# One more buffer for the routing tiles, and two bias tiles staged in the token-row buffers

## The chip, the cores and the metric

The kernel runs on 1 core of one Trainium2 chip. The metric is the device time of one execution in microseconds (us). The time before is 1835.21 us, the median of 3 runs (1820.68, 1835.21 and 1837.70).

## The reference, cut to what matters

One layer over 512 tokens of width 1024: a mixer (sparse attention and a state-space branch), then a mixture of 32 experts, 4 for each token. The change lies where the mixer ends and the experts begin.

```python
logits = (hf @ w_router + b_router).astype(jnp.float32)
top_val, top_idx = lax.top_k(logits, TOP_K)           # 4 of 32 experts per token
gates = jax.nn.softmax(top_val, axis=-1)
...
xb = h_pad[toks]                                      # the rows of one expert, in blocks of 128
gu = xb @ w_gu[e] + b_gu[e]
g, u = gu[:, :D_EXPERT], gu[:, D_EXPERT:]
g = jnp.minimum(g, SWIGLU_LIMIT)
u = jnp.clip(u, -SWIGLU_LIMIT, SWIGLU_LIMIT)
act = (u + 1.0) * (g * jax.nn.sigmoid(SWIGLU_ALPHA * g))
out = act @ w_dn[e] + b_dn[e]                         # times the row's gate, then summed by token
...
x = x + g_f * moe
```

The last line's bias part does not need the experts' rows: for each token it is the sum over experts of gate times `b_dn[e]`, that is `gates @ b_dn`. The kernel computes it once for all four tiles of 128 tokens. These are the "shared-bias tiles".

## The kernel before, in words

All weights stream from HBM in tiles of 128x2048 f32 (1 MB). SyncE issues each load as soon as its buffer is free; there are ten buffers (six `raw2`, `B0`, `B1`, two `raw`). Each weight tile is split in two fp32r tiles by `msplit`: `hi` on ScalarE (L1318), `lo = raw - hi` on VectorE (L1319). A product is made of three matmuls (hi by hi, lo by hi, hi by lo; L1496 to L1498, for expert 0 L1353 to L1355). One expert takes 12 weight tiles: for each half f of its width two tiles for the gate half of `gu`, two for the up half, and two for a half of the down product.

For each expert e, GpSimd gathers its 128 rows of `h2d` in a tile `xg` (L1376, two buffers), by the indices `gi`; TensorE transposes them (L1270, `tr<-cst,xg`), ScalarE and VectorE make the hi and lo parts (`xh` L1271, `xl` L1273). After the gate and up products VectorE clips `u` (L1285) and makes `act` (L1286); TensorE transposes `act` (L1270, `tr<-cst,act`) for the down product. The down product of expert e-1 runs between the products of expert e; its result `y` (L1556, tag `y`, two buffers) is added to the output in HBM by an indirect accumulating DMA (`put`, L1289) with the row indices `si`.

The indices come from a routing step, done for groups of experts: `[0]`, `[1, 2]`, `[3]`, `[4..7]`, `[8..11]` and so on. Each group leaves four small tiles: `q`, `gi`, `si` and `gate`, allocated with the tags of the same names and `bufs=nbuf + 1`, which is 3 here. `si` of a group is read until the last `put` of its experts has landed. The group `[4..7]` is the fourth to be allocated and takes the buffer of group `[0]`; its `si` is written (L1248) at the end of the loop pass for e = 1, in which expert 0's `put` is issued.

The shared-bias tiles: `shared_biases` (L1390) loads `b_dn` to a `y` buffer and makes from it and the gates the two operands; `shared_down(t, ...)` (L1411) makes tile t: two matmuls (L1417, `dn<-ah,al`), two VectorE products with `gf` (L1418, `y<-dn,gf`), and one accumulating DMA to the output (L1419, `out_dram<-y`). Four tiles pass through the two `y` buffers, so tile 2 and tile 3 are written when the DMAs of tile 0 and 1 have landed. The row buffers `xg` are allocated in the order of the gathers: expert 0 in the first, expert 1 in the second, expert 2 in the first again.

What sets the order: a planner (the tile framework) puts the instructions of every engine in a fixed order when the kernel is built. It takes the earliest in program order among those that its own estimates hold to be ready. Within the loop over experts 1 to 32 the order on TensorE, VectorE and ScalarE is written out by hand (`tc.manual_schedule`); GpSimd's queue is the planner's throughout, and so is all of expert 0's part, which it may interleave with the beginning of expert 1's. On the chip every engine takes its instructions in that order and waits at each for what it needs.

In each hand-ordered pass for expert e and half f stand, in this order: gate product, a routing step, up product (with `u` and `act`), the transposes of half f of the next expert's rows, a routing step, the first half of the down product, the transposes of `act`, the second half of the down product.

`cmb` and `cmt` are two 128x128 bf16 mask tiles of the mixer, held in the pool `con` that lives to the end. The pool `W` lives as long as the mixer; the experts' pool `M` is placed on the memory that `W` leaves.

Of the kernel before, what the change touches and what calls it, by code (L numbers as in the profile page):

```python
# [13 lines left out]
BF = mybir.dt.bfloat16  # L14
I32 = mybir.dt.int32
# [7 lines left out]
P = 128  # L23
L = 512
NT = L // P
# [108 lines left out]
def program(tc, A, dbg=None, upto=99):  # L134
# [5 lines left out]
    with ctx:  # L140
# [15 lines left out]
            (0, 8), (8, 24), (24, 32), (32, 38), (38, 46), (46, 106), (106, 114)))  # L156
        identb = con.tile([P, P], BF, name="identb")
        V.tensor_copy(identb, ident)
        cmb = con.tile([P, P], BF, name="cmb")
        V.tensor_copy(cmb, cmask)  # L160
        ones = con.tile([P, P], F32, name="ones")
        V.memset(ones, 1.0)
        aux = con.tile([P, NT, NE, 6], BF, name="aux")
# [43 lines left out]
        with ExitStack() as c1:  # L207
# [53 lines left out]
            def weave(*lists, at=None):  # L261

                steps = [((i + (at[n] if at else 0.5)) / len(ls), n, i) for n, ls in enumerate(lists) for i in range(len(ls))]
                for _, n, i in sorted(steps):
                    lists[n][i]()


            def two(tag):
# [447 lines left out]
                    V.tensor_scalar(mask[:, qt - 1, 0:n], sc, -2e38, NEG, op0=OP.is_gt, op1=OP.mult)  # L716


            cmt = con.tile([P, P], BF, name="cmt")
            V.tensor_scalar(cmt, trile, -1.0, -NEG, op0=OP.add, op1=OP.mult)  # L720
            sts = big("V", [P, 4, L])
            v3 = lambda a: a.rearrange("p (h d) -> p h d", d=64)
# [501 lines left out]
        def block_parts(M, mp, nbuf):  # L1224
            def mt(shape, dt=F32, name="t", bufs=None):
                return M.tile(list(shape), dt, name=name, tag=name, bufs=bufs or nbuf)

            def picked(hots, name, bufs, c):
                n = len(hots)
                p = mp.tile([P, 512], F32, name=name, tag=name, bufs=bufs)[:, 0:3 * n].rearrange("p (e c) -> p e c", c=3)  # L1230
                for i, (hot, aux_of) in enumerate(hots):
                    for t in range(NT):
                        T.matmul(p[:, i, :], hot[:, t, :], aux_of(t)[:, c:c + 3], start=(t == 0), stop=(t == NT - 1))
                return p.rearrange("p e c -> p c e")

            def slots(hots):

                n = len(hots)
                q = mt([P, 8, n], name="q", bufs=nbuf + 1)
                V.tensor_copy(q[:, 0:3, :], picked(hots, "mi", 1, 0))  # L1240
                return rows_of(q, n)

            def rows_of(q, n):
                gi, si = mt([P, n], I32, name="gi", bufs=nbuf + 1), mt([P, n], I32, name="si", bufs=nbuf + 1)
                V.scalar_tensor_tensor(q[:, 6], q[:, 0], 128.0, q[:, 1], op0=OP.mult, op1=OP.add)
                V.tensor_copy(gi, q[:, 6])
                V.tensor_scalar(q[:, 7], q[:, 2], cm512, c512, op0=OP.mult, op1=OP.add)
                V.tensor_tensor(si, q[:, 6], q[:, 7], op=OP.add)  # L1248
                return q, gi, si

            def share(hots, q):
                V.tensor_copy(q[:, 3:6, :], picked(hots, "dn", 2, 3))
                return share_of(q, len(hots))

            def share_of(q, n):
                gate = mt([P, n], name="gate", bufs=nbuf + 1)
                V.tensor_tensor(gate, q[:, 3], q[:, 4], op=OP.add)
                V.tensor_tensor(gate, gate, q[:, 5], op=OP.add)
                return gate

            def transposed(src, name, split_=True, b=None, into=None, scale=1.0):
                if into is None:
                    hi = mt([P, KD, P], F32R if split_ else F32, name=name + "h", bufs=nbuf)
                    lo = mt([P, KD, P], F32R, name=name + "l", bufs=nbuf) if split_ else None
                else:
                    hi, lo = into
                for b in range(2) if b is None else (b,):
                    p = mp.tile([P, 4, P], F32, name="tr", tag="tr", bufs=2)
                    for k in range(4):
                        T.transpose(p[:, k, :], src[:, (4 * b + k) * P:(4 * b + k + 1) * P], ident)  # L1270
                    S.activation(hi[:, 4 * b:4 * b + 4, :], p, AF.Copy, scale=scale)  # L1271
                    if split_ and scale == 1.0:
                        V.tensor_tensor(lo[:, 4 * b:4 * b + 4, :], p, hi[:, 4 * b:4 * b + 4, :].bitcast(F32),  # L1273
                                        op=OP.subtract)
                    elif split_:
                        V.scalar_tensor_tensor(lo[:, 4 * b:4 * b + 4, :], p, scale,
                                               hi[:, 4 * b:4 * b + 4, :].bitcast(F32), op0=OP.mult, op1=OP.subtract)
                return hi, lo

            def gated(act, p):  # L1280
                S.activation(act, p, AF.Silu, scale=ALPHA)

            def upped(u, p, act):

                V.tensor_scalar(u, p, 8.0, -6.0, op0=OP.min, op1=OP.max)  # L1285
                V.scalar_tensor_tensor(act, act, SILU7, u, op0=OP.min, op1=OP.mult)  # L1286

            def put(y, si, out=out):
                return G.indirect_dma_start(out=out, out_offset=bass.IndirectOffsetOnAxis(ap=si, axis=0), in_=y,  # L1289
                                     in_offset=None, compute_op=OP.add)  # L1290

            def all_picked(p, i, hot, aux_of):
                for t in range(NT):
                    T.matmul(p[:, i, :], hot[:, t, :], aux_of(t), start=(t == 0), stop=(t == NT - 1))

            def all_of(p, n):
                q = mt([P, 8, n], name="q", bufs=nbuf + 1)
                V.tensor_copy(q[:, 0:6, :], p.rearrange("p e c -> p c e"))
                q, gi, si = rows_of(q, n)
                return gi, si, share_of(q, n)  # L1300

            return slots, share, transposed, gated, upped, put, all_picked, all_of

        with ExitStack() as c2:
# [19 lines left out]
            def mt(shape, dt=F32, name="t", bufs=2):  # L1324
                return M.tile(list(shape), dt, name=name, tag=name, bufs=bufs)
# [17 lines left out]
            def three(x, b, e, c0, tag, bufs):  # L1343

                p = mp.tile([P, 512], F32, name=tag, tag=tag, bufs=bufs)
                if b is not None:
                    half, c = divmod(c0, b.shape[1])
                    T.matmul(p, sel2[:, half, e:e + 1].to_broadcast([P, P]), b[:, c:c + 512], start=True, stop=False)
                for i in range(2):
                    hi, lo = weights()  # L1350
                    for k in range(4):
                        ws, kk = slice(k * 512, (k + 1) * 512), 4 * i + k
                        T.matmul(p, x[0][:, kk, :], hi[:, ws], start=(b is None and kk == 0), stop=False)  # L1353
                        T.matmul(p, x[0][:, kk, :], lo[:, ws], start=False, stop=False)
                        T.matmul(p, x[1][:, kk, :], hi[:, ws], start=False, stop=(kk == KD - 1))  # L1355
                return p
# [30 lines left out]
            def sized(name):  # L1387
                return spare[name].pop(0) if spare[name] else mt([P, D], name=name, bufs=2 if name == "y" else 1)
# [21 lines left out]

            def shared_down(t, gT, b):  # L1411

                y = sized("y")
                for n in range(2):
                    ns = slice(n * 512, (n + 1) * 512)
                    p = mp.tile([P, 512], F32, name="dn", tag="dn", bufs=2)
                    T.matmul(p, gT[:, t, :], b[:, ns], start=True, stop=True)  # L1417
                    V.tensor_tensor(y[:, ns], p, gf[:, ns], op=OP.mult)  # L1418
                G.dma_start(out[t * P:(t + 1) * P, :], y, accum_op=OP.add)  # L1419
# [33 lines left out]
            for f in range(2):  # L1453
                fs = slice(f * 512, (f + 1) * 512)
                u = mt([P, 512], name="u", bufs=1)
                gated(act[:, fs], three(xT, bias["b_gu"], 0, f * 512, "gu", 3))
                if f == 0:
                    shares()
                    gates_of([0])
                    gates_of(groups[0])  # L1460
                    for step in routed([3]):
                        step()
                upped(u, three(xT, bias["b_gu"], 0, FE + f * 512, "gu", 3), act[:, fs])
                if f == 0:
                    shared = shared_biases()
                    xT_next = transposed(xg, "x")
                    xg = gather(2)
                else:
                    for t in range(NT):
                        shared_down(t, *shared)  # L1470
                aT = transposed(act, "a", b=f, into=aT, scale=1.0 / ALPHA)
            few = mt([P, NE], name="few", bufs=1)
# [208 lines left out]
```

## Time and profile before

| | us |
|---|---|
| median of 3 runs | 1835.21 |
| the three runs | 1820.68, 1835.21, 1837.70 |
| the profiled execution | 1834.64 |
| its span, from first to last instruction | 1832.9 |
| TensorE busy | 1764.1 (96%) |
| VectorE busy | 1542.3 (84%) |
| ScalarE busy | 1074.0 (59%) |
| GpSimd busy | 194.1 (11%) |
| data moved by DMA | 527.24 MB, mean 288 GB/s |

The profiled execution's own time is 1.7 us above its span and 0.6 us below the median. The mixer takes about the first 620 us, expert 0 and the start of expert 1 some 70 us more, and from about 740 us on the experts follow one another at about 36 us each until the end. In the rows below PE is TensorE, DVE VectorE, ACT ScalarE, POOL GpSimd and SP SyncE; times are us from the start of the span. The idle time in brackets is that of the engine just before the instruction, with what released it.

### The profile page before, as it was taken

The page shows a single profiled execution, that of the slowest core. Times are in us where ns is not written, and L with a number is a line of the kernel's source. Part 1 is how long each engine was busy: PE and PEld are TensorE (multiplying, and loading weights), DVE is VectorE, ACT ScalarE, POOL GpSimd, SP SyncE. Part 2 cuts the span into 40 slices and gives each one's busy share as a digit, 9 for nine tenths or more (in the row PEclk, how much of TensorE's full clock was granted, in tenths as well). Part 3 has the DMA queues.
Part 4 walks back from the last instruction along what each step waited for, and adds up shares of the span by engine and source line. Part 5 has one row for each costly group of instructions (what it writes and reads, how often), then busy time and mean ns, then how long its engine had stood idle before and what let it go on. Part 6 is the DMA issues. An engine that isn't in the chain of part 4 may idle for free.

```text
span 1832.9 us, 22584 instructions
## 1 busy us (share of the span) xinstructions
PE 1764.1 (96%) x8536; PEld 1392.0 (76%) x8536; DVE 1542.3 (84%) x1886; ACT 1074.0 (59%) x1059; POOL 194.1 (11%) x115
## 2 busy tenths in 40 slices
PE   7999999999999788999999999999999999999997
PEld 3866877776778566787888888888888788788885
DVE  6486678875776787999999999999999999999996
ACT  3443433444323365677777777777677777777774
POOL 0000000000000110111211111111111111211112
PEclk9988999998899899999999999999999999999999
DMA  8242334432575588999999999999999999999993
GB/s 327 71 150 72 117 134 165 152 126 76 200 262 197 192 288 286 361 378 374 373 381 375 380 363 390 372 382 369 369 384 386 352 396 379 358 385 381 377 354 73
DMA packets 86599, 527.24 MB, mean 288 GB/s; under 512 B 10928, under 2 KB 11088, under 8 KB 32216
## 3 DMA queue, kind: packets, MB, share of 16 engines
q1 hardware_dynamic: 70552, 469.70, 66.4%
q0 software_dynamic: 15696, 55.97, 11.2%
q8 instruction: 68, 1.11, 0.2%
q14 instruction: 43, 0.35, 0.1%
q10 hardware_dynamic: 240, 0.10, 0.0%
HBM read 497.91 MB, written 30.45 MB: 288 GB/s over the span
## 4 chain that ended last, share of the span: by engine, by line
PE 86%; DVE 8%; DMA 3%; issue 2%; ACT 1%; POOL 0%; SPq 0%; DVEq 0%; POOLq 0%; ACTq 0%
PE gu L1498 12%; PE gu L1496 12%; PE gu L1497 12%; PE dn L1496 6%; PE dn L1498 6%; PE dn L1497 6%; PE mm L392 4%; PE mm L393 4%; PE mm L394 4%; PE tr L1270 3%; PE gu L1507 2%; PE ac L849 1%; PE at L821 1%; PE mm L384 1%; DVE wlo L1319 1%
## 5 line engine op out<-in xcount | busy, mean ns | idle before, releaser
L1319 DVE TENSOR_TENSOR wlo<-raw,whi 128x2048 fp32r<-128x2048 f32 x154 | 352.1, 2287 | 30.1 <-ACT whi L1318 30.0
L1319 DVE TENSOR_TENSOR mlo<-raw,mhi 128x2048 fp32r<-128x2048 f32 (+1 forms) x160 | 352.5, 2207 | 25.2 <-ACT mhi L1318 22.9
L1318 ACT ACTIVATE whi<-raw 128x2048 fp32r<-128x2048 f32 x154 | 296.1, 1923 | 128.3 <-PE gu L1498 68.0
L1318 ACT ACTIVATE mhi<-raw 128x2048 fp32r<-128x2048 f32 (+1 forms) x160 | 296.0, 1855 | 104.7 <-PE gu L1498 58.4
L1498 PE MATMUL gu<-whi,xl 128*128 128x512 f32 x496 | 196.2, 396 | 0.0
L1497 PE MATMUL gu<-wlo,xh 128*128 128x512 f32 x496 | 196.0, 395 | 0.0
L1496 PE MATMUL gu<-whi,xh 128*128 128x512 f32 x496 | 195.8, 395 | 0.0
L1496 PE MATMUL gu<-mhi,xh 128*128 128x512 f32 x496 | 193.7, 390 | 0.0
L1497 PE MATMUL gu<-mlo,xh 128*128 128x512 f32 x496 | 193.7, 390 | 0.0
L1498 PE MATMUL gu<-mhi,xl 128*128 128x512 f32 x496 | 193.6, 390 | 0.0
L1289 POOL DMA_INDIRECT out_dram<-y,si x30 | 100.7, 3358 | 445.1 <-DVE y L1556 445.1
L393 PE MATMUL mm<-B,whi 128*128 128x512 f32 x352 | 142.0, 404 | 0.0
L392 PE MATMUL mm<-bA,whi 128*128 128x512 f32 x320 | 132.1, 413 | 2.0 <-DVE brow L661 1.0
L394 PE MATMUL mm<-bA,wlo 128*128 128x512 f32 x320 | 129.0, 404 | 0.8 <-DVE wlo L185 0.8
L184 ACT ACTIVATE whi<-raw 128x2048 fp32r<-128x2048 f32 x34 | 64.9, 1913 | 88.2 <-PE mm L393 69.6
L1376 POOL DMA_INDIRECT xg<-h2d,gi x32 | 57.7, 1802 | 537.6 <-PE tr L1270 496.3
L1497 PEld LDWEIGHTS gu<-wlo,xh 128*128 128x128 f32 x496 | 93.2, 188 | 22.4
L1498 PEld LDWEIGHTS gu<-whi,xl 128*128 128x128 f32 x496 | 93.2, 188 | 22.3
L1496 PEld LDWEIGHTS gu<-whi,xh 128*128 128x128 f32 x496 | 93.3, 188 | 21.3
L1496 PE MATMUL dn<-whi,ah 128*128 128x512 f32 x256 | 108.1, 422 | 1.4 <-DVE y L1418 1.4
L1497 PE MATMUL dn<-wlo,ah 128*128 128x512 f32 x256 | 103.4, 404 | 5.7 <-DVE wlo L1319 5.7
L1497 PEld LDWEIGHTS gu<-mlo,xh 128*128 128x128 f32 x496 | 93.1, 188 | 20.1
(471 smaller groups left out, 3687.7 us busy)
## 6 DMA issues: line engine op xcount, KB each, us to landing
raw<-in_w_gu_dram SPq DMA_DIRECT2D x204, 1024.0 KB
raw<-in_w_dn_dram SPq DMA_DIRECT2D x104, 1024.0 KB
B<-in_w_gu_dram SPq DMA_DIRECT2D x52, 1024.0 KB
B<-in_w_dn_dram SPq DMA_DIRECT2D x24, 1024.0 KB
raw<-in_w_in_dram SPq DMA_DIRECT2D x23, 1024.0 KB
rawp<-in_w_ada_dram POOLq DMA_DIRECT2D x30, 512.0 KB, 4.2
bE<-in_w_ada_dram SPq DMA_DIRECT2D x4, 1024.0 KB
bC<-in_x_dram SPq DMA_DIRECT2D x8, 512.0 KB
```

The costliest lines, as they stand in the source:

```text
L184: S.activation(hi[:, 0:n], raw[:, 0:n], AF.Copy)
L392: T.matmul(p, wh, xT[0][:, k, :], start=(k == 0), stop=False)
L393: T.matmul(p, wh, xT[1][:, k, :], start=False, stop=False)
L394: T.matmul(p, wl, xT[0][:, k, :], start=False, stop=(k == nk - 1))
L1270: T.transpose(p[:, k, :], src[:, (4 * b + k) * P:(4 * b + k + 1) * P], ident)
L1289: return G.indirect_dma_start(out=out, out_offset=bass.IndirectOffsetOnAxis(ap=si, axis=0), in_=y, in_offset=None, compute_op=OP.add)
L1318: S.activation(hi[:, cs], raw[:, cs], AF.Copy)
L1319: i = V.tensor_tensor(lo[:, cs], raw[:, cs], hi[:, cs].bitcast(F32), op=OP.subtract)
L1376: G.indirect_dma_start(out=xg, out_offset=None, in_=h2d, in_offset=bass.IndirectOffsetOnAxis(ap=info[e][0], axis=0))
L1496: T.matmul(p, x[0][:, kk, :], hi[:, ws], start=(start and kk == 0), stop=False)
L1497: T.matmul(p, x[0][:, kk, :], lo[:, ws], start=False, stop=False)
L1498: T.matmul(p, x[1][:, kk, :], hi[:, ws], start=False, stop=(kk == KD - 1))
```

## The change

The tags `q`, `gi`, `si` and `gate` get a fourth buffer. The first two shared-bias tiles are written to buffers of the tag `xg` in place of `y`; they and the gather for expert 2 behind them now stand, in program order, between expert 0's gate and up products of the second half (f = 1). In the first half the gather for expert 2 is taken out. The `xg` buffers are thus taken in the order expert 0, expert 1, bias tile 0, bias tile 1, expert 2, expert 3. The other two bias tiles keep their place and use `y` buffers. The masks `cmb` and `cmt` move from `con` to `W`, and the copy that makes `cmb` stands some lines later.

```diff
-        cmb = con.tile([P, P], BF, name="cmb")
-        V.tensor_copy(cmb, cmask)
...
+            cmb = W.tile([P, P], BF, name="cmb")
+            V.tensor_copy(cmb, cmask)
...
-            cmt = con.tile([P, P], BF, name="cmt")
+            cmt = W.tile([P, P], BF, name="cmt")
...
-                q = mt([P, 8, n], name="q", bufs=nbuf + 1)
+                q = mt([P, 8, n], name="q", bufs=nbuf + 2)
...
-                gi, si = mt([P, n], I32, name="gi", bufs=nbuf + 1), mt([P, n], I32, name="si", bufs=nbuf + 1)
+                gi, si = mt([P, n], I32, name="gi", bufs=nbuf + 2), mt([P, n], I32, name="si", bufs=nbuf + 2)
...
-                gate = mt([P, n], name="gate", bufs=nbuf + 1)
+                gate = mt([P, n], name="gate", bufs=nbuf + 2)
...
-                y = sized("y")
+                y = mt([P, D], name="xg", bufs=2) if t < 2 else sized("y")
...
                 gated(act[:, fs], three(xT, bias["b_gu"], 0, f * 512, "gu", 3))
+                if f:
+                    for t in range(2):
+                        shared_down(t, *shared)
+                    xg = gather(2)
...
                     xT_next = transposed(xg, "x")
-                    xg = gather(2)
                 else:
-                    for t in range(NT):
+                    for t in range(2, NT):
                         shared_down(t, *shared)
```

## Rows read from the trace of the kernel before

**Rows 1.** Busy time by stretch: us and instruction count per engine, PEclk, DMA share, GB/s.
```profile
680.00:700.00 20.00, 14.59 (x53) 10.93 (x54) 17.90 (x16) 6.95 (x6) 1.68 (x2) 0.74 1.02 310
...
800.00:1000.00 200.00, 199.82 (x926) 161.79 (x925) 187.13 (x135) 143.08 (x100) 28.05 (x11) 1.00 1.00 377
```

**Rows 2.** Timeline of PE, expert 1's first half: start, duration, line, tiles, idle before.
```profile
676.27 0.60 PE L1270 MATMUL tr<-cst,xg 128*128 128x128 f32 x4
681.38 1.39 PE L1417 MATMUL dn<-ah,al 128*128 128x512 f32 x2 [4.51 <-DVE y L1418]
...
691.12 1.08 PE L1270 MATMUL tr<-cst,act 128*128 128x128 f32 x4 [2.61 <-DVE act L1286]
```

**Rows 3.** Timeline of DVE over the same stretch.
```profile
663.97 2.29 DVE L1319 TENSOR_TENSOR wlo<-raw,whi 128x2048 fp32r<-128x2048 f32 x1
...
671.84 0.68 DVE L1418 TENSOR_TENSOR y<-dn,gf 128x512 f32<-128x512 f32 x1
...
680.63 1.29 DVE L1418 TENSOR_TENSOR y<-dn,gf 128x512 f32<-128x512 f32 x2 [2.30 <-DMA out_dram<-y]
683.36 1.29 DVE L1418 TENSOR_TENSOR y<-dn,gf 128x512 f32<-128x512 f32 x2 [1.44 <-DMA out_dram<-y]
...
690.28 0.69 DVE L1286 SCALAR_TENSOR_TENSOR act<-act,u 128x512 f32<-128x512 f32 x1
```

**Rows 4.** Timeline of PE in expert 2's first half, and the same place one half later.
```profile
726.00 0.60 PE L1270 MATMUL tr<-cst,xg 128*128 128x128 f32 x4
...
732.51 0.80 PE L1497 MATMUL dn<-wlo,ah 128*128 128x512 f32 x1 [5.68 <-DVE wlo L1319]
...
738.42 0.63 PE L1270 MATMUL tr<-cst,act 128*128 128x128 f32 x4 [0.85 <-DVE act L1286]
...
753.22 0.60 PE L1270 MATMUL tr<-cst,xg 128*128 128x128 f32 x4
...
756.46 0.60 PE L1270 MATMUL tr<-cst,act 128*128 128x128 f32 x4
```

**Rows 5.** Timeline of DVE at the end of the pass for expert 1.
```profile
729.82 0.16 DVE L1248 TENSOR_TENSOR si<-q 128x4 int32<-128x4 f32 x1 [9.78 <-DMA out_dram<-y,si]
```

**Rows 6.** Waits by engine: us in total, times, longest; 800 to 1000 us.
```profile
ACT mhi L1318 <- PE gu L1498: 15.0, 18, 1.2
```

**Rows 7.** Timeline of SP's queue and of ACT: one weight buffer's loads, then its splits.
```profile
767.52 3.29 SPq L953 DMA_DIRECT2D B<-in_w_gu_dram  x2
...
792.67 1.92 ACT L1318 ACTIVATE mhi<-B 128x2048 fp32r<-128x2048 f32 x1 [0.83 <-PE dn L1498]
```

**Rows 8.** Timeline of POOL: gather for expert 2, stores of bias tiles 0 and 3, expert 0's put.
```profile
642.61 0.96 POOL L1376 DMA_INDIRECT xg<-h2d,gi  x1 [0.30 <-issue]
...
674.03 0.97 POOL L1419 DMA_DIRECT2D out_dram<-y  x1 [6.97 <-DVE y L1418]
...
685.23 0.84 POOL L1419 DMA_DIRECT2D out_dram<-y  x1 [2.17 <-DVE y L1418]
...
717.20 3.38 POOL L1289 DMA_INDIRECT out_dram<-y,si  x1 [31.13 <-DVE y L1556]
```

**Rows 9.** DMA issues at 664.65, 674.03 and 717.20: last number, us from issue to landing.
```profile
xg<-h2d,gi POOLq DMA_INDIRECT x1, 7.9
...
out_dram<-y POOLq DMA_DIRECT2D x1, 512.0 KB, 6.5
...
out_dram<-y,si POOLq DMA_INDIRECT x1, 12.5
```

**Rows 10.** Busy time by stretch, columns as in Rows 1: after each of PE's two idle times.
```profile
684.20:688.52 4.32, 4.32 (x12) 3.11 (x12) 4.32 (x4) 0.00 (x0) 0.84 (x1) 0.67 1.06 208
691.12:694.40 3.28, 3.28 (x11) 2.80 (x12) 3.28 (x4) 0.60 (x1) 0.00 (x0) 0.58 1.00 415
```

**Rows 11.** Timeline of ACT and of DVE: the first weight splits in the experts' pool.
```profile
621.67 3.69 ACT L1318 ACTIVATE mhi<-raw 128x2048 fp32r<-128x2048 f32 x2
...
628.93 4.49 DVE L1319 TENSOR_TENSOR mlo<-raw,mhi 128x2048 fp32r<-128x2048 f32 x2
```

More of the change, by code (lines that the diff above doesn't have):

```diff
@@ L1296, in all_of @@
             def all_of(p, n):
-                q = mt([P, 8, n], name="q", bufs=nbuf + 1)
+                q = mt([P, 8, n], name="q", bufs=nbuf + 2)
                 V.tensor_copy(q[:, 0:6, :], p.rearrange("p e c -> p c e"))
```

## The prediction

> **What bounds the kernel now.** I read the busy time by stretch first, to see where TensorE is the bound and where not; then the timelines of TensorE and VectorE in the stretches where it is not; then the list of waits and the DMA landings. From 800 to 1000 us TensorE is busy 199.82 of 200 us at a granted clock of 1.00 (the level of 2.4 GHz) [rows 1]. What ScalarE waits for there is TensorE, which frees the split buffers, and no wait for a weight load stands in that list [rows 6]. So from there to the end TensorE sets the time, and what is won before is won at the end, if the weights come as much earlier.
>
> They can. Two loads to the B buffers are issued from 767.52 on, and the first of them is split at 792.67, 25.2 us later, when TensorE has freed the split buffer [rows 7]. The change wins a bit over half of that at most, and since a load is issued when its buffer is freed by a split, the loads move with TensorE.
>
> Two stretches near the change are not TensorE's. From 680 to 700 us it is busy 14.59 of 20 us at a clock of 0.74, while VectorE has 17.90 [rows 1]. Here TensorE waits 4.51 us before the matmuls of bias tile 3, and 2.61 us for `act` before its transposes at 691.12 [rows 2]. VectorE had stood still 2.30 and 1.44 us before its products for tiles 2 and 3, until the accumulating DMAs of tiles 0 and 1 had landed and left the `y` buffers [rows 3]. The second place is 726 to 738 us: TensorE waits 5.68 us for a `lo` tile [rows 4], because VectorE stood still 9.78 us before writing `si` of experts 4 to 7 [rows 5]. That is the buffer of group [0], read by expert 0's put, which was issued at 717.20 [rows 8] and took 12.5 us to land [rows 9]: 717.20 + 12.5 = 729.7.
>
> **Part 1, the fourth buffer.** Group [4..7] takes a fresh buffer, so the wait of 9.78 us goes. What is late next is what is always late: in the undisturbed expert that follows, TensorE goes from the transposes of the rows (753.22) to those of `act` (756.46) in 3.24 us; here it took 738.42 - 726.00 = 12.42 us [rows 4]. That difference holds the idle time, a second wait of 0.85 us, and the matmuls at the lower clock. The gain is 12.42 - 3.24 = **9.2 us**. No later group can wait in its place: group [8..11] takes the first buffer again one group of four experts later, when expert 0's put has long landed. Without the stall VectorE reaches 726 us with the two `lo` tiles of this down product done, as it does one expert later. The lower bound is the 5.68 us of idle time alone; I take the upper, since the same instructions stand in both stretches. The fourth buffers of `q`, `gi` and `gate` add no instruction.
>
> **Part 2, the bias tiles in `xg`.** No instruction is added: eight matmuls, eight products and four stores remain, but in another order. What goes is VectorE's 2.30 + 1.44 = 3.74 us of standing still. VectorE is the engine that TensorE waits for at 691.12, so `act`, which ends at 690.28 + 0.69 = 690.97 [rows 3], could end at 687.2, and the transposes of `act` could begin at 691.12 - 3.74 = 687.4.
>
> What is added is a wait: the gather for expert 2. Before, it was issued at 642.61 [rows 8] and had landed long before its rows were transposed at 676.27 [rows 2]. Now it has to wait until bias tile 0 has left the first `xg` buffer. Queued behind it on GpSimd are what the planner puts there, the stores of tiles 2 and 3 and the gather for expert 3, which nobody needs soon (the rows of expert 3 are transposed at 726.00 [rows 4]). Queued behind its reader, the transposes at 676.27, is all of TensorE's work: the first half of the down product and then the transposes of `act`.
>
> When does it land? In program order tile 0 now stands behind the weight split that ends at 663.97 + 2.29 = 666.26 [rows 3], and ahead of the two that follow. With one instruction of the same width ahead of the two products, at 0.68 us each [rows 3], tile 0 is done at 666.26 + 3 x 0.7 = 668.4. The store follows some 0.6 us behind (683.36 + 1.29 = 684.65 against the issue at 685.23 [rows 3, 8]), at 669.0. It lands 6.5 us later [rows 9], at 675.5; the gather takes 7.9 us [rows 9] and lands at 683.4. Then come four transposes, 0.60 us [rows 2], and twelve matmuls of the down product, which took 4.32 us right after an idle time [rows 10]: the transposes of `act` can begin at 688.3. That is later than VectorE's 687.4, so the new wait takes back 0.9 us and decides. The shift is 691.12 - 688.3 = 2.8 us.
>
> To this comes the clock. After its idle time of 2.61 us TensorE ran the stretch 691.12 to 694.40 at 0.58 [rows 10], near the lower level (1.2 GHz). At 688.3 it would come straight from 4.9 us of matmuls, in which, as in the same twelve before, the clock has come back up; 3.28 x (1 - 0.58) = 1.4 us are won. Part 2 gives 2.8 + 1.4 = **4.2 us**. Its bounds: 3.74 + 1.4 = 5.1 us if the gather comes early enough, and less than nothing if tile 0 is not moved ahead on VectorE (the first rival).
>
> For a plain store of 512 KB issued by GpSimd the Trainium skill, page "DMA: Bandwidth & Descriptors", section "Anatomy of one DMA — SWDGE (gpsimd) path", has a fit of 2.0 us plus the bytes at 436 GB/s, from which I estimate 3.2 us; the store here, which accumulates, showed 6.5 us [rows 9], and the measured number is used. By the page's figure part 2 would give 5.1 us.
>
> **Part 3, the masks.** The two casts stay among VectorE's first instructions. The `M` tiles may lie over other `W` tiles than before and wait for other readers. The first that matter are the splits at 621.67 on ScalarE, whose VectorE half begins at 628.93 [rows 11]: the first of the two could come 628.93 - 621.67 - 1.85 = 5.4 us later without moving it. I take nothing, and 1 us at most either way.
>
> **The sum.** 9.2 + 4.2 = 13.4 us, from 1834.64: 1821.2 us. The median of the runs is 0.6 us above the profiled execution, so **1822 us** (-0.7%).
>
> **Rivals.** First, **one wait for another**. The planner may leave tile 0's products where they were, behind the two later splits: then its first product is at 671.84 and its store at 674.03 as before [rows 3, 8]. It lands at 680.5, the gather at 688.4, the transposes of `act` follow 4.9 us behind at 693.3. Part 2 then costs 2.2 us and gives 1.4 us of clock back: -0.8. The total is 8.4 us, 1834.64 - 8.4 + 0.6 = 1827. For it speaks that the order of expert 0's part is the planner's; against it that tile 0 now stands ahead of those two splits in program order.
>
> Second, on the **slower side: the gather behind the stores**. GpSimd's queue is the planner's. If it puts the gather for expert 2 behind the store of tile 3 and that queue is held until this has landed, the gather is issued at 685.23 + 6.5 = 691.7 [rows 8, 9], lands at 699.6, and the transposes of `act` begin at 704.5: 13.4 us lost, 1.4 of clock and 9.2 of part 1 won, 2.8 us slower, 1838. The point at which it decides: each microsecond by which expert 2's rows come after 683.4 is lost on TensorE, so the kernel is slower once they land after 683.4 + 13.4 = 696.8. Against it: program order has only tiles 0 and 1 ahead of the gather.
>
> Third, **the DMA engines are the bound**. Their share is 1.00 from 800 to 1000 us, at 377 GB/s [rows 1]. If that is all they can move, TensorE gets ahead and then waits for weights, and the time stays at 1835. Against it stands the 25.2 us between issue and use [rows 7], and that no engine waits for a load. The Trainium skill, page "Perfetto Trace Analysis", section "What \"DMA-bound\" means", counts a kernel as DMA-bound when particular DMA engines are; by that the share of 1.00 speaks for this rival, while the waits of this trace do not agree.
>
> Fourth, **the spread of the runs**: one of the three lies 14.5 us under the median, for a reason that the one trace cannot show. If the runs of the changed kernel mostly fall like that one, the median is 1820.68 - 13.4 = 1807.
>
> **How the numbers follow.** The forecast has 0.50, one wait for another 0.25, the gather behind the stores 0.05, the DMA bound 0.07, the lower group of runs 0.13. The range must leave out no more than 0.2: from 1807 to 1833 us it leaves out the second and third rivals, 0.12. About 1% (18.4 us) is what a measurement of this kernel tells from no change. Only the fourth case is faster by more: 0.13, and 0.02 for a larger part 2. The slower side needs a gather 18 us later still: 0.03. Within 1%: 0.82.
>
> **What would show it.** Right: no wait of VectorE before the `si` of experts 4 to 7, none before the bias products on a DMA, TensorE without an idle time between the transposes of expert 2's and 3's rows, and one idle time before the transposes of expert 2's rows that ends with the gather, at about 683. Wrong: if that idle time is longer than 7 us, if VectorE's products of tile 0 come behind the splits, if TensorE shows waits for `lo` tiles that wait for weight loads later on, or if another wait of VectorE stands at the end of expert 1's pass.

## The result, and the profile after

| | before | after |
|---|---|---|
| median of the runs, us | 1834.01 (1820.68 to 1837.70, 4 runs) | 1814.36 (1812.58 to 1818.29, 4 runs) |
| ratio, 95% interval | | 0.9900 (0.9873 to 0.9927) |
| the profiled execution | 1834.64 | 1815.36 |
| its span | 1832.9 | 1813.6 |
| TensorE busy in it | 1764.1 | 1752.4 |

The changed kernel is about 1% faster, 19.65 us by the medians and 19.3 by the spans, where 13.4 were forecast. In a later series it took 1809.95 us beside 1833.15 (ratio 0.9871, 0.9848 to 0.9894). Lines after the change lie one to four further down: L1270 is L1271, L1286 is L1287, L1417 to L1419 are L1418 to L1420, L1496 to L1498 are L1500 to L1502.

The timeline of TensorE after the change, at the places of [rows 2, 4], with the first transposes of rows ahead of them:

```profile
636.09 1.97 PE L1271 MATMUL tr<-cst,xg 128*128 128x128 f32 x8 [9.68 <-DMA xg<-h2d,gi]
...
674.60 0.50 PE L1501 MATMUL gu<-mlo,xh 128*128 128x512 f32 x1 [1.46 <-DVE mlo L1320]
...
685.84 1.09 PE L1271 MATMUL tr<-cst,xg 128*128 128x128 f32 x4 [4.81 <-DMA xg<-h2d,gi]
...
690.62 0.60 PE L1271 MATMUL tr<-cst,act 128*128 128x128 f32 x4
...
723.92 0.60 PE L1271 MATMUL tr<-cst,xg 128*128 128x128 f32 x4
...
727.15 0.60 PE L1271 MATMUL tr<-cst,act 128*128 128x128 f32 x4
```

The reader is to see four things. Before the transposes of expert 2's rows (685.84) there is now one idle time, 4.81 us, and it ends with the gather. Behind it nothing waits for `act`. From 723.92 to 727.15 it takes 3.23 us, without the 5.68 us of idle time that stood there [rows 4]. And there is a new wait that the forecast did not have, 1.46 us for `mlo` at 674.60, because VectorE now makes the bias products ahead of these splits; it costs nothing, since TensorE waits for the gather behind it in any case.

The same from VectorE's side; the row of `si` has no idle time in brackets, against 9.78 us [rows 5]:

```profile
669.24 1.28 DVE L1419 TENSOR_TENSOR xg<-dn,gf 128x512 f32<-128x512 f32 x2
...
672.27 4.48 DVE L1320 TENSOR_TENSOR mlo<-raw,mhi 128x2048 fp32r<-128x2048 f32 x2
...
689.26 0.69 DVE L1287 SCALAR_TENSOR_TENSOR act<-act,u 128x512 f32<-128x512 f32 x1
...
718.23 0.16 DVE L1249 TENSOR_TENSOR si<-q 128x4 int32<-128x4 f32 x1
```

GpSimd's queue: the store of bias tile 0, the gather for expert 2 that waits for it, the gather for expert 3, the stores of tiles 2 and 3 and expert 0's put:

```profile
670.82 0.93 POOL L1420 DMA_DIRECT2D out_dram<-xg  x1 [26.07 <-DVE xg L1419]
...
677.08 1.04 POOL L1377 DMA_INDIRECT xg<-h2d,gi  x1 [3.57 <-DMA out_dram<-xg]
679.82 0.98 POOL L1377 DMA_INDIRECT xg<-h2d,gi  x1 [1.70 <-PE tr L1271]
680.79 1.97 POOL L1420 DMA_DIRECT2D out_dram<-y  x2
715.35 3.39 POOL L1290 DMA_INDIRECT out_dram<-y,si  x1 [32.59 <-DVE y L1560]
```

Tile 0 stands ahead of the splits, as the forecast had it, and the gather is behind the stores of tiles 0 and 1 alone. The DMA landings of that store and that gather (last number, us from issue to landing; the gather's at 677.08):

```profile
out_dram<-xg POOLq DMA_DIRECT2D x1, 512.0 KB, 5.5
...
xg<-h2d,gi POOLq DMA_INDIRECT x1, 8.6
```

Now the sum over the spans, from one mark to the next (us; before from [rows 2, 4] and the row at 633.37 below):

| stretch | before | after | won | forecast |
|---|---|---|---|---|
| start to the first transposes of rows (expert 0) | 633.4 | 636.1 | -2.7 | 0 |
| to the transposes of `act`, expert 1, first half | 57.75 | 54.53 | 3.2 | 2.8 |
| to the transposes of expert 2's second half of rows | 34.88 | 33.30 | 1.6 | 1.4 |
| to the transposes of `act` behind them | 12.42 | 3.23 | 9.2 | 9.2 |
| to the end | 1094.5 | 1086.45 | 8.0 | 0 |
| sum | 1832.9 | 1813.6 | 19.3 | 13.4 |

Three terms came out near what was worked out; the experiments show how much of that agreement is luck. A fourth, nearly as large as the largest, was not in the forecast: the 30 experts that follow, in which the change alters no instruction, take 8.0 us less. Busy time by stretch, from the fourth mark to the end, first before, then after (us, then busy time and number of instructions of TensorE, its weight loads, VectorE, ScalarE, GpSimd, then clock, DMA share and GB/s):

```profile
738.42:1832.90 1094.48, 1082.83 (x4990) 877.08 (x4990) 1012.08 (x748) 768.91 (x538) 157.23 (x60) 1.00 0.97 362
```

```profile
727.15:1813.60 1086.45, 1074.68 (x4991) 874.61 (x4990) 1011.67 (x748) 770.44 (x538) 158.92 (x60) 1.00 0.97 366
```

The first row of the table is not the change's: it lies ahead of the mark from which the forecast counts. From that mark to the end the changed kernel takes 1177.5 us in place of 1199.5, which is 22.0 less, and its execution in the later series takes 1177.5 as well (628.24 to 1805.7).

Behind the fourth mark TensorE's idle time is the same, 11.65 and 11.77 us, and so are its number of instructions and its clock. The matmuls themselves are shorter: 1082.83 against 1074.68, 8.15 us. Which ones is seen in the groups by line from 800 to 1760 us (busy time, mean ns of one), before:

```profile
L1496 PE MATMUL gu<-mhi,xh 128*128 128x512 f32 x429 | 167.5, 390 | 0.0
...
L1496 PE MATMUL gu<-whi,xh 128*128 128x512 f32 x418 | 165.0, 395 | 0.0
...
L1498 PE MATMUL dn<-whi,al 128*128 128x512 f32 x216 | 85.4, 395 | 0.0
```

and after:

```profile
L1500 PE MATMUL gu<-whi,xh 128*128 128x512 f32 x430 | 168.0, 391 | 0.0
...
L1500 PE MATMUL gu<-mhi,xh 128*128 128x512 f32 x424 | 165.7, 391 | 0.0
...
L1502 PE MATMUL dn<-whi,al 128*128 128x512 f32 x211 | 83.4, 395 | 0.0
```

Before, the gate and up matmuls on the weight tiles `whi` and `wlo` took 395 ns and those on `mhi` and `mlo` 390, with the same shape and type. After, both take 391. The down matmuls stay at 395.

### The profile page after: what moved, and what is told of

It is laid out like the page before. It is cut to its first block, busy times and chain, and to the rows that moved or that the text cites. A ratio compares the mean times of both kernels' runs of the same rounds, so it can differ in the third digit from the quotient of the medians.

```text
span 1813.6 us, 22580 instructions
## 1 busy us (share of the span) xinstructions
PE 1752.4 (97%) x8534; PEld 1389.9 (77%) x8536; DVE 1542.5 (85%) x1886; ACT 1074.8 (59%) x1059; POOL 196.4 (11%) x115
## 4 chain that ended last, share of the span: by engine, by line
PE 88%; DVE 6%; DMA 3%; ACT 2%; issue 1%; SPq 0%; POOLq 0%; DVEq 0%; ACTq 0%
PE gu L1502 12%; PE gu L1500 12%; PE gu L1501 12%; PE dn L1500 7%; PE dn L1502 7%; PE dn L1501 6%; PE mm L393 4%; PE mm L394 4%; PE mm L395 4%; PE tr L1271 3%; PE gu L1511 2%; PE ac L850 1%; PE at L822 1%; DMA xg<-h2d,gi 1%; PE mm L385 1%
## 5 line engine op out<-in xcount | busy, mean ns | idle before, releaser
L1502 PE MATMUL gu<-whi,xl 128*128 128x512 f32 x496 | 193.8, 391 | 0.0
L1500 PE MATMUL gu<-mhi,xh 128*128 128x512 f32 x496 | 193.8, 391 | 0.0
L1502 PE MATMUL gu<-mhi,xl 128*128 128x512 f32 x496 | 193.8, 391 | 0.0
L1500 PE MATMUL gu<-whi,xh 128*128 128x512 f32 x496 | 193.8, 391 | 0.0
L1502 PEld LDWEIGHTS gu<-mhi,xl 128*128 128x128 f32 x496 | 93.1, 188 | 20.2
L1502 PEld LDWEIGHTS gu<-whi,xl 128*128 128x128 f32 x496 | 93.1, 188 | 20.2
L1500 PEld LDWEIGHTS gu<-mhi,xh 128*128 128x128 f32 x496 | 93.1, 188 | 19.5
L1500 PEld LDWEIGHTS gu<-whi,xh 128*128 128x128 f32 x496 | 93.1, 188 | 19.3
```

Source lines behind the costliest of these rows:

```text
L1500: T.matmul(p, x[0][:, kk, :], hi[:, ws], start=(start and kk == 0), stop=False)
```

## The experiments

**The placement theory.** A fourth buffer of `q` (8 x 4 values of 4 bytes), `gi` and `si` (16 bytes, each placed in 32) adds 128 + 32 + 32 = 192 bytes per partition ahead of the row buffers in the pool `M`; one of `gate` adds 32 between `xl` and `ah`. All tiles placed behind them move, the operands `xh`, `xl`, `ah` and `al` and the split tiles `mhi` and `mlo` among them; `whi` and `wlo` lie in front and keep their place modulo 256 bytes. Before, `whi` minus `xh` was 192 bytes modulo 256 and `mhi` minus `xh` 0; after, both are 0 (`wlo`, `mlo` and `xl` lie whole multiples of 256 from these). `ah` lay 96 bytes from `whi` and 160 from `mhi`, after it 128 from both. (These are the addresses that the built kernels give the tiles.) The theory: a matmul is faster when its two operands lie a multiple of 256 bytes apart. The rival: the fourth buffers take a small wait out of every group of experts.

Four kernels each do one thing alone; they were timed on one chip beside 25 runs of the kernel before (median 1832.75).

**The fourth buffers alone.** The `bufs=nbuf + 2` lines of the change and nothing else.

> The kernel before with the fourth buffer of q, gi, si and gate alone; the bias tiles and the masks as before. By the prediction's part 1 the wait before the si of experts 4 to 7 goes and 9.2 us with it. The address theory (the 8.0 us that the changed kernel won after the predicted places come from the gate and up matmuls on whi and wlo, 391 ns in place of 395, because the 192 bytes of the three new buffers ahead of xg move xh and xl against whi and wlo from 192 to 0 bytes modulo 256) adds 8.0 us: 17.2 us faster, with 390 to 391 ns for these matmuls. The rival (the 8.0 us belong to the bias tiles, to the masks or to the spread of the runs) gives 9.2 us and 395 ns.

Measured 1815.49 us (1811.65 to 1816.63), ratio 0.9894 (0.9863 to 0.9925): 17.3 us faster by the medians. Timeline of TensorE and busy time by stretch:

```profile
634.29 1.97 PE L1270 MATMUL tr<-cst,xg 128*128 128x128 f32 x8 [9.86 <-DMA xg<-h2d,gi]
...
691.88 0.63 PE L1270 MATMUL tr<-cst,act 128*128 128x128 f32 x4 [1.47 <-DVE act L1286]
...
725.25 0.60 PE L1270 MATMUL tr<-cst,xg 128*128 128x128 f32 x4
...
728.49 0.60 PE L1270 MATMUL tr<-cst,act 128*128 128x128 f32 x4
```

```profile
728.49:1814.80 1086.31, 1074.66 (x4991) 874.68 (x4990) 1011.88 (x748) 770.23 (x538) 158.86 (x60) 1.00 0.97 366
```

3.24 us between the transposes, and 1074.66 us of matmuls from there on: both the stall and the unforeseen 8 us belong to this part of the change.

The trace shows one thing more. From the transposes of `act` to those of expert 2's second half of rows it takes 725.25 - 691.88 = 33.37 us, against 34.88 before [rows 2, 4], though the bias tiles are as they were. TensorE waits 1.47 us for `act` in place of 2.61, and behind this wait its clock is at the upper level. Busy time by stretch behind that wait, before and here:

```profile
691.12:707.61 16.49, 16.49 (x75) 13.13 (x75) 15.26 (x12) 8.79 (x6) 0.00 (x0) 0.92 0.99 341
```

```profile
691.88:706.97 15.09, 15.09 (x74) 12.10 (x75) 15.00 (x12) 9.29 (x7) 0.00 (x0) 1.00 0.98 364
```

So the clock's 1.4 us of the forecast's part 2 are gone here without part 2. On top of the fourth buffers the bias tiles win only (691.88 - 634.29) + 33.37 - 54.53 - 33.30 = 3.1 us, not 4.2. Why the clock came out higher here is not shown.

**192 unused bytes alone.** The kernel before, with a tile that nobody uses at the place where the new buffers lie:

```diff
             route([0])
+            pad = mt([P, 48], name="pad", bufs=1)
             xg = gather(0)
```

> The kernel before with nothing but an unused tile of 192 bytes in the experts' pool ahead of xg, which moves xh and xl against whi and wlo from 192 to 0 bytes modulo 256 as the changed kernel does. Address theory: 8.0 us faster, gate and up matmuls on whi and wlo at 390 to 391 ns in place of 395, both stalls as before. Rival (the 8.0 us come from the order, the buffers or the spread of the runs): no change, 395 ns.

Measured 1827.68 us (1822.36 to 1830.88), ratio 0.9977 (0.9952 to 1.0001). Timeline and busy time by stretch:

```profile
725.49 0.60 PE L1270 MATMUL tr<-cst,xg 128*128 128x128 f32 x4
...
738.71 0.63 PE L1270 MATMUL tr<-cst,act 128*128 128x128 f32 x4 [0.85 <-DVE act L1286]
```

```profile
738.71:1826.20 1087.49, 1075.90 (x4990) 875.01 (x4990) 1012.01 (x748) 770.51 (x538) 159.05 (x60) 1.00 0.97 365
```

The stall is still there (13.22 us between the transposes), yet the matmuls of the rest take 1075.90 us in place of 1082.83. No buffer was added that anything could wait for, so the rival falls. The 1.2 us that are still missing to 1074.68 are about what the down matmuls cost at 160 bytes in place of 128 (table below). The whole time alone, 5.1 us less, would not have told it from no change; the busy time does.

**The bias tiles alone** (the last three pieces of the diff).

> The kernel before with the bias tiles 0 and 1 in the xg buffers and the later gather for expert 2 alone; three routing buffers, masks as before. Prediction, part 2: the transposes of act come some 3 us earlier against the first transposes of expert 0, and with the clock 4 to 5 us are won; whi and wlo lie against xh as before, so 395 ns remain: 4.2 to 5 us faster. Rival (the bias tiles also bring the 8.0 us): 12 to 13 us faster, 391 ns. Rival (one wait for another): within 1 us of before.

Measured 1829.56 us (1827.52 to 1831.59), ratio 0.9978 (0.9964 to 0.9991). Timeline of TensorE:

```profile
632.87 1.97 PE L1270 MATMUL tr<-cst,xg 128*128 128x128 f32 x8 [9.69 <-DMA xg<-h2d,gi]
...
683.01 1.04 PE L1270 MATMUL tr<-cst,xg 128*128 128x128 f32 x4 [4.78 <-DMA xg<-h2d,gi]
...
687.84 0.60 PE L1270 MATMUL tr<-cst,act 128*128 128x128 f32 x4
...
721.43 0.60 PE L1270 MATMUL tr<-cst,xg 128*128 128x128 f32 x4
```

and of the kernel before, its mark ahead of [rows 2]:

```profile
633.37 1.97 PE L1270 MATMUL tr<-cst,xg 128*128 128x128 f32 x8 [9.53 <-DMA xg<-h2d,gi]
```

From the first transposes to those of `act` it takes 54.97 us in place of 57.75, and from there 33.59 in place of 34.88: 2.8 + 1.3 = 4.1 us, where 2.8 + 1.4 = 4.2 were forecast. TensorE is busy 1082.71 us from 733.00 on, as before, so this part has no share in the 8 us:

```profile
733.00:1827.30 1094.30, 1082.71 (x4990) 876.61 (x4990) 1012.14 (x748) 769.20 (x538) 157.38 (x60) 1.00 0.97 362
```

**The masks alone** (the first three pieces).

> The kernel before with the two masks in the mixer's pool alone: the weight tiles and the experts' pool both move down by 512 bytes and keep their distance. Prediction, part 3, and address theory: no change (within 1 us by the stretches of the trace), 395 ns. Rival (the place of the weight tiles by itself makes the matmuls faster, or the masks cost something in the mixer): 8 us faster with 391 ns, or slower in the first 620 us.

Measured 1834.43 us (1830.36 to 1839.23), ratio 1.0006 (0.9989 to 1.0023), and 1082.83 us of matmuls in the rest, as before. Nothing, as forecast:

```profile
737.96:1832.60 1094.64, 1082.83 (x4990) 876.58 (x4990) 1012.14 (x748) 769.05 (x538) 157.39 (x60) 1.00 0.97 362
```

**The distance put back.** The fourth buffers alone with 64 unused bytes more, so that `whi` and `xh` lie 192 bytes apart again:

```diff
             route([0])
+            pad = mt([P, 16], name="pad", bufs=1)
```

> The fourth routing buffers alone, with an unused tile of 64 bytes more ahead of the row buffers, so that the 192 new bytes become 256 and the activations' tiles keep their old place to the whi and wlo tiles modulo 256 bytes (192 bytes apart, as before). Placement theory: the gate and up matmuls on whi and wlo are back at 395 ns, an expert takes 36.27 us, and only the stall's 9.2 us are won: 1823.5, not the 1815.5 of the fourth buffers alone. Rival: the fourth buffers save the 8 us in some other way (a wait taken away in every group of experts): then it stays at 1815.5 with 390 ns or with shorter idle times.

Measured 1824.43 us (1822.31 to 1826.16), ratio 0.9947 (0.9929 to 0.9966), against 1815.49 without the pad. Groups by line:

```profile
L1497 PE MATMUL gu<-whi,xh 128*128 128x512 f32 x424 | 167.3, 395 | 0.0
L1497 PE MATMUL gu<-mhi,xh 128*128 128x512 f32 x424 | 165.7, 391 | 0.0
...
L1498 PE MATMUL dn<-wlo,ah 128*128 128x512 f32 x215 | 84.0, 391 | 0.0
...
L1498 PE MATMUL dn<-mlo,ah 128*128 128x512 f32 x211 | 83.1, 394 | 0.0
```

The fourth buffers are there and serve, and 64 bytes that nobody reads take the gain of the gate and up matmuls away: 395 ns on `whi` again. That the distance decides holds: neither tile's own place does, since before the change the same `xh` ran at two paces, and `whi`, which the 192 unused bytes did not move, changed its pace. The stretch behind the wait for `act` took 33.54 us here, short as with the fourth buffers alone. But the down matmuls on `wlo`, now 64 bytes from `ah`, fell to 391, which a rule of the multiple alone does not give. So the distances were varied in the changed kernel, the whole series beside seven runs of the kernel before on each of two chips.

**All operands a multiple of 256 apart.** With a pad ahead of `ah`:

```diff
+                pad = mt([P, 32], name="pad", bufs=1)
                 b = mt([P, KD, P], F32R, name="ah").rearrange("p k c -> p (k c)")
```

> The changed kernel once more, on the same chip as the version with aligned tiles: 1814 (1812 to 1818), gate and up matmuls at 390 to 391 ns, down matmuls at 394 to 396 ns (those that begin a chunk 415).

> The changed kernel with an unused tile of 128 bytes ahead of the activations' tiles ah and al, so that these too stand at a multiple of 256 bytes from all four weight tiles (before 128 off). Placement theory: the 48 down matmuls of an expert fall from 394 to 396 ns to 390, as the gate and up matmuls did at the same distance; those took 8.0 us less in all over 48 matmuls per expert, so this takes another 8 us: 1806, faster than both kernels. Rival (the gate and up matmuls became faster for another reason than the distance to their operand): 1814 and 394 to 396 ns.

Measured 1811.34 us (1810.76 to 1812.73), ratio 0.9875 (0.9859 to 0.9892), beside 1809.95 us (1806.78 to 1812.80) for the changed kernel. Groups by line and busy time by stretch of the aligned one:

```profile
L1501 PE MATMUL gu<-whi,xh 128*128 128x512 f32 x432 | 169.0, 391 | 0.0
...
L1503 PE MATMUL dn<-whi,al 128*128 128x512 f32 x209 | 81.9, 392 | 0.0
L1502 PE MATMUL dn<-wlo,ah 128*128 128x512 f32 x209 | 81.4, 390 | 0.0
```

```profile
725.91:1810.10 1084.19, 1071.67 (x4991) 873.57 (x4990) 1011.24 (x748) 770.51 (x538) 158.92 (x60) 1.00 0.97 367
```

The down matmuls did fall, to 390 to 392 ns (the first of each three, `dn<-whi,ah` and `dn<-mhi,ah`, from 415 and 416 to 414 and 413), but all matmuls together take only 3.0 us less (1074.68 - 1071.67), not 8, and the whole time shows no gain over the changed kernel. The down matmuls gained 3.3 ns each (table below), not 5, since at 128 they had been 1 ns faster than before; and the gate and up matmuls became 0.3 ns slower. No version here beats the changed kernel in whole time.

**Other distances**, each with one execution: pads of 160 and of 96 bytes at that place, and one of 192 bytes ahead of `xh`.

> The changed kernel with an unused tile of 160 bytes there: the tiles ah and al stand 224 bytes from a multiple of 256 away from the weight tiles (32 short of it). If only the exact multiple counts, the down matmuls stay at 394 to 396 ns; if nearness counts, they fall in part, to 391 to 393 ns. Rival as above: no change at any distance.

> The changed kernel with ah and al 32 bytes from a multiple of 256 away from the weight tiles, on the other side than the run at 224. If the exact multiple counts, the down matmuls are at 394 to 396 ns as at 224; if the distance of 64 bytes that ran at 391 to 394 ns on the whi and wlo tiles is the sign of a graded effect, 390 to 392.

> The changed kernel with an unused tile of 192 bytes ahead of xh: the gate and up products' operands 64 bytes apart modulo 256 in place of 0, the down products' 192 in place of 128. If 64 is as good as 0: gate and up matmuls at 390 to 391 ns on all four weight tiles, 36.0 us per expert. If only 0 is good: 394 to 396 ns on all four, twice as many slow ones as in the kernel before, 36.5 us per expert, and 1828 to 1832 in all.

The last took 1824.01 us, with 1080.98 us of matmuls in the rest; the other two 1812.61 and 1814.56. The table has the mean time from one matmul's start to the next one's inside a product, from 800 to 1760 us (gaps over 0.3 us left out), by the distance between the starts of the weight tile and of the activations' tile modulo 256 bytes, over all kernels of this study:

| distance, bytes | gate and up, ns | down, ns |
|---|---|---|
| 0 | 227.9 to 228.4 | 229.2, 229.5 |
| 32 | | 232.8, 233.0 |
| 64 | 230.0 | 229.5 |
| 96 | | 233.5 to 233.7 |
| 128 | | 232.2 to 232.7 |
| 160 | | 233.5 to 233.9 |
| 192 | 233.1 | 233.2 |
| 224 | | 232.9, 233.0 |

Both expectations for the gate and up matmuls at 64 bytes miss: 64 is neither as good as 0 nor as bad as 192. Nearness does not count either: 32 and 224 are slow.

**Only bias tile 0 in a row buffer.** The gather for expert 2 then waits for no store:

```diff
-                y = mt([P, D], name="xg", bufs=2) if t < 2 else sized("y")
+                y = mt([P, D], name="xg", bufs=2) if t < 1 else sized("y")
```

> The changed kernel with only bias tile 0 staged in a row buffer, tile 1 in y again; the gather for expert 2 then takes expert 1's buffer and waits for no store. Theory (the landing of that gather decides by less than 1 us, VectorE is next): TensorE's idle time of 4.81 us before the transposes of expert 2's rows goes, and a wait of about 4 us for act stands before the transposes of act, which come where VectorE lets them, at most 0.7 us earlier than in the changed kernel, with up to 1.4 us lost to the clock: no difference in the whole time (1810 to 1816). Rival (the gather alone sets this place): the transposes of act come 4 us earlier, at 49 to 51 us after the first transposes of rows in place of 54.5.

Measured 1813.62 us (1809.83 to 1815.47), ratio 0.9896 (0.9879 to 0.9912). Its timeline of TensorE, and busy time by stretch behind the last row:

```profile
673.13 0.60 PE L1271 MATMUL tr<-cst,xg 128*128 128x128 f32 x4
...
675.96 0.50 PE L1501 MATMUL dn<-wlo,ah 128*128 128x512 f32 x1 [2.00 <-DVE wlo L1320]
...
682.38 1.08 PE L1271 MATMUL tr<-cst,act 128*128 128x128 f32 x4 [3.60 <-DVE act L1287]
```

```profile
682.38:700.07 17.69, 17.69 (x74) 14.08 (x75) 15.28 (x12) 8.77 (x6) 0.00 (x0) 0.84 1.01 394
```

The same stretch of the changed kernel, 690.62 to 705.67, holds the same work and takes 15.05 us; its clock is 1.00:

```profile
690.62:705.67 15.05, 15.05 (x75) 12.07 (x74) 14.49 (x12) 10.57 (x7) 0.00 (x0) 1.00 1.02 389
```

The gather's wait is gone, and 5.6 us of waits for VectorE stand in its place. The transposes of `act` come 682.38 - 628.49 = 53.89 us after the first transposes, against 54.53: 0.6 us earlier, as the theory had it. Then TensorE pays 2.6 us for its lower clock behind the second idle time, not 1.4. From the first transposes to the end this execution takes 1179.5 us against 1177.5, a difference that the whole time does not show. In these two executions it matters less which wait stands there than where: the changed kernel's idle time lies ahead of the down product's first half, and the clock is back up before the transposes of `act`.

## Why the prediction was right, and what it lacked

**Part 1, 9.2 us for the stall: right.** 3.23 us from transposes to transposes against a forecast 3.24, and no other wait on VectorE took its place. That the gain agrees to a tenth is in part luck: it is counted from the same trace that gave the forecast, and in the four executions that keep the stall it takes 11.4, 11.6, 12.4 and 13.2 us.

**Part 2, 4.2 us: right in its path, with luck in its sizes.** Counted from the first transposes (633.37 before), the gather was to land 50.0 us on; TensorE took its rows at 685.84 - 636.09 = 49.75. Four errors cancelled there. The store was issued 0.9 us earlier than worked out (34.7 us on, against 35.6) and was 1.0 us faster (5.5 us for 6.5); the gather was issued 0.8 us after the store had landed, where the forecast had nothing between them, and was 0.7 us slower (8.6 for 7.9). The estimate of 3.2 us that the prediction takes from the Trainium skill (page "DMA: Bandwidth & Descriptors", section "Anatomy of one DMA — SWDGE (gpsimd) path") is below this store's 5.5 us too. That the gather decides, and VectorE is next by less than 1 us, the run with one tile in a row buffer shows. The clock's term measured 1.3 us by the bias tiles alone (34.88 - 33.59), but about as much went with the fourth buffers alone (33.37), so it can't be put down to part 2. Of the 3.2 and 1.6 us in the table, 0.4 and 0.3 us lie between the changed kernel and the bias tiles alone (54.97 and 33.59 us); matmuls on `whi` and `wlo` stand in both stretches, and I put this down to their distance, without a run that isolates it.

**Part 3, nothing: right.**

**The rivals.** One wait for another and the gather behind the stores did not come: tile 0's products stood ahead of the splits (669.24 against 672.27), the gather ahead of the stores of tiles 2 and 3. The DMA bound did not either: from the fourth mark on, the same loads go through at 366 GB/s in place of 362, with TensorE's idle time unchanged; from 800 to 1760 us, at a share of 1.00 in both, at 379 in place of 376. The Trainium skill's section that the prediction cites (page "Perfetto Trace Analysis", section What "DMA-bound" means) counts particular DMA engines among what a kernel can be bound on; here a share of 1.00 [rows 1] was no such bound. The fourth, the spread of the runs, was real in kind. Two executions of the changed kernel make their first transposes at 636.09 and here, in the later series:

```profile
628.24 1.97 PE L1271 MATMUL tr<-cst,xg 128*128 128x128 f32 x8 [9.64 <-DMA xg<-h2d,gi]
```

Their spans are 1813.6 and 1805.7: 7.85 us apart at the start of the experts and 7.9 at the end. So the spread between these two comes out of the mixer; what in it varies was not tried. In the profiled execution after the change it cost 2.7 us. Over the thirteen executions profiled here the first transposes come between 628.24 and 638.82 us.

**What was missing: 8.0 us, the largest error.** The step that failed is the last sentence of part 1, "the fourth buffers of `q`, `gi` and `gate` add no instruction", taken as a cost of nothing, with part 3's "I take nothing" for tiles that come to lie elsewhere. New buffers move every tile behind them, and I had weighed what a moved tile might wait for, but not what it does to the pace of the matmuls that read it. That they are sensitive could be read before the change: the groups by line show one form of matmul at 390 ns on `mhi` and 395 on `whi`. The forecast of 1822 thus had the three parts that it named right in sum and came out 7.6 us too high (1814.36). These 8 us are also what carried the change to about 1%, where the forecast had it at 0.7%, and the range down to 1807 held them only because it had been drawn for the lower group of runs: that is luck.

Still open is why 0 bytes and, for the down products, 64 are fast, and whether the weight load and the matmul meet in the memory: the runs show the pace by distance, not its cause.

## What to carry to other kernels

Cost a new buffer also by the tiles that it moves: where a profile shows one form of instruction at two durations by operand, the placement is at work, and one unused tile tries it. Judge such small effects by the busy time of a stretch with equal instruction counts, which agreed within 0.2 us among four executions whose spans lay up to 9 us apart (1805.7 to 1814.8: the changed kernel twice, the fourth buffers alone, and one bias tile in a row buffer). Where the stretches ahead of the change vary, count from a mark behind them. When a wait can't be removed, put it where TensorE has matmuls that need nothing else between it and the next wait; here that was worth 2.0 us, in one execution each.

## What the runs showed of the hardware

Gate and up matmuls (128x512, fp32r, granted clock 1.00) followed one another at 227.9 to 228.4 ns when the moving tile (the weights) and the stationary tile (the activations) start a multiple of 256 bytes apart, and at 233.1 when they lie 192 from one (2.2%). From the fourth mark to the end there are some 3 x 418 x 1094.5 / 960 = 1,430 gate and up matmuls on `whi` and `wlo`; 5.0 ns each are 7.2 us, and 1.1 ns on each of about as many down matmuls (233.7 at 96 and 160 bytes, 232.6 at 128) 1.6 us: 8.8, near the 8.15 measured. With one bias tile in a row buffer, TensorE's idle times of 2.00 and 3.60 us, with 2.8 us of matmuls between them, left it at a granted clock of 0.84 over the next 17.69 us. In the changed kernel, with the one idle time of 4.81 us and 4.78 us of transposes and matmuls behind it, the stretch that follows was at 1.00. With the fourth buffers alone it was at 1.00 behind a wait of 1.47 us, and before at 0.92 behind one of 2.61 us.
